# Input scaling of two layers moved to VectorE alone, norm vector loaded first, index heads paired with zero-padded keys

## The chip, the core and the metric

The kernel runs on one core of one Trainium2 chip. The metric is the device time of one execution in microseconds. The kernel before takes 2158.25 us (median of three executions, 2156.83 to 2161.36).

The engines of the core have these names in the profile: PE multiplies matrices (PEld are its weight loads), DVE is VectorE, ACT is ScalarE, POOL is GpSimd, SP issues most transfers.

## The reference

Input is one sequence of 256 tokens with 2048 features in fp32. Two layers follow each other. Each normalizes its input, makes one wide projection, runs two token mixers side by side, multiplies each by a gate, projects back and adds the result to the input.

```python
def layer_ab(x, ...):
    h = rms_norm(x, norm_g)                       # x * rsqrt(mean(x*x)) * gain
    proj = einsum('btd,de->bte', h, w_in)
    q, k, v, o_pre, z_a, i_pre, f_pre, z_b, xbc, dt_raw = split_cols(proj, SPLIT_AB)
    y = concatenate([mlstm_branch(...), mamba2_branch(...)])
    return x + einsum('bte,ed->btd', y, w_out)

def layer_cd(x, ...):
    h = rms_norm(x, norm_g)
    proj = einsum('btd,de->bte', h, w_in)
    q_c, ckv, z_c, iq, ik, iw, qkv, z_d, b_pre, a_pre = split_cols(proj, SPLIT_CD)
    y = concatenate([dsa_branch(...), gdn_branch(...)])
    return x + einsum('bte,ed->btd', y, w_out)
```

Inside `dsa_branch` every query scores all keys with 16 index heads of 64 features: `score = einsum('bqhd,bsd->bqhs', iq, ik)`, and `index = einsum('bqh,bqhs->bqs', iw, relu(score))` picks the keys that attention sees. `gdn_branch` is a gated delta rule over chunks of 64 tokens whose output is normalized head by head. A last rms_norm ends the program.

## The kernel before, in words

**Products in three parts.** Every projection keeps fp32 precision by splitting both operands into a high and a low part. A weight piece `wr` (four blocks of 128 rows by 512 columns, called a group here) arrives by DMA on SP's queue into one of three buffers. ACT casts it to `wh` (L191), DVE subtracts that from `wr` to get `wl` (L192); there are two buffers of each. The layer's input is held the same way in `hT`, transposed: 16 blocks k of 128 features, each with 256 high and 256 low columns. A product takes three matmuls for each pair of row block and column block: wh by high, wh by low, wl by high (`proj_feat`). A group is 48 such matmuls of 256 columns.

**What sets the order.** Small work is written as generators in the list `steps`. `tick()` advances the first of them by one `yield` and is called after each quarter of a group; `lag(n)` lets n ticks pass; `flush()` ticks until the list is empty. PE instructions issued inside a tick keep their place in program order, all others are placed by the tile scheduler by priority.

**The layer's input.** `normed()` turns the residual `xr` by PE (`xt`, L79), multiplies by the gain into `xg` (L306 on ACT, L308 on DVE), casts to the high half of `hT` (ACT, L295) and subtracts for the low half (L296: DVE for even pairs of blocks, POOL for odd). The squares are summed meanwhile (L323 on ACT, L325 on DVE), the inverse root is taken in 12 tiny DVE instructions (L141 to L147), spread over all partitions by `dg` (L333) and a product `rbp` with ones, and copied to `rb` (L335). The first product of a layer works on the unscaled `hT`, and its result is multiplied by `rb` when it leaves PSUM (L411 in layer 1, L747 in layer 2). After LR = 10 ticks the step `rescaled()` scales `hT` for all later products: eight times a DVE multiply of a pair of blocks (L315), an ACT cast (L295) and a POOL subtraction (L296). The first product of layer 1 is `bc_half(0)`, in groups of 1, 1, 2, 4, 4 and 4 blocks; after it come the gates' product, `bc_half(1)` and the other column blocks. In layer 2 the first is half of the index queries (CIQ, i = 0), then the other half.

**The other places.** `index()` computes the scores of one head a tick: two matmuls with the head's 64 features as contraction (128 and 256 columns). `delta()` ends with the normalization of the delta rule's output `og` on DVE (L1266), a lag of LT = 4 ticks and the turn of `og` by PE (L79). The turn of the normalized latent `cn` (L932) stands in the list without a lag. Matmuls `pw` have 64 columns of stationary operand.

## Time and profile before

| what | value |
|---|---|
| median of three executions | 2158.25 us (2156.83 to 2161.36) |
| profiled execution | 2157.74 us |
| its span, first to last instruction | 2156.0 us |
| PE busy | 2107.7 us, 98% |
| DVE, ACT, POOL busy | 1467.5, 993.7, 149.6 us |
| mean granted TensorE clock | 0.992 |

The page gives the busy time of each engine; the view of waits lists what the engine stood idle for; windows give the same busy times for chosen stretches with the granted clock (1.00 is the upper of the two levels, 0.50 the lower, values between are mixtures); the timeline lists runs of equal instructions with their start, and in brackets the idle time ahead of them and what ended it. Times count from the start of the span.

### The profile page before, as it was taken

How to read it: one execution, taken by the hardware profiler on the slowest of the kernel's cores; microseconds unless marked ns; L12 is line 12 of the kernel's file. 1: busy time of each engine (PE TensorE's matmuls, PEld its weight loads, DVE VectorE, ACT ScalarE, POOL GpSimd, SP SyncE). 2: the span in 40 equal slices, each digit the busy share in tenths (PEclk: the TensorE clock that was granted, in tenths of full speed). 3: DMA queues.
4: the chain of work that ended last, by engine and by line, in shares of the span. 5: the costliest groups of instructions: out<-in, count | busy, mean ns of one | idle time of the engine just before them, and what ended most of it. 6: DMA issues, size and time to landing. Idle time of an engine off the chain costs nothing.

```text
span 2156.0 us, 31526 instructions
## 1 busy us (share of the span) xinstructions
PE 2107.7 (98%) x12878; PEld 1861.2 (86%) x12878; DVE 1467.5 (68%) x2096; ACT 993.7 (46%) x1311; POOL 149.6 (7%) x168
## 2 busy tenths in 40 slices
PE   7999999999999999899999999999999999999997
PEld 6989997888889788898878888899898988989986
DVE  7888764555455456578979998555666666766765
ACT  5455443334433444355643333455444444444543
POOL 4000020000000000300100002000000000000001
PEclk9999999999999999999999999999999999999999
DMA  6565456555555555576886666755565555565543
GB/s 184 190 212 176 157 179 215 195 176 176 176 184 187 176 187 185 139 237 221 296 229 202 224 204 207 265 181 181 176 233 180 190 172 189 188 195 182 171 160 124
DMA packets 242342, 415.16 MB, mean 193 GB/s; under 512 B 45093, under 2 KB 69206, under 8 KB 240342
## 3 DMA queue, kind: packets, MB, share of 16 engines
q1 hardware_dynamic: 237254, 389.84, 55.4%
q0 software_dynamic: 4944, 23.31, 3.3%
q8 instruction: 101, 1.65, 0.3%
q14 instruction: 43, 0.35, 0.0%
HBM read 389.87 MB, written 26.38 MB: 193 GB/s over the span
## 4 chain that ended last, share of the span: by engine, by line
PE 85%; DVE 6%; ACT 3%; issue 1%; DMA 1%; ACTq 0%; SPq 0%
PE pt L75 49%; PE pf L75 27%; DVE wl L192 3%; ACT wh L191 2%; PE turn L79 1%; PE py L75 1%; PE pu L75 1%; PE si L75 1%; ACT Dt L862 1%; PE po L75 0%; PE lgt L75 0%; PE num L75 0%; PE pog L75 0%; DMA Dt<-gd 0%; PE vt L79 0%
## 5 line engine op out<-in xcount | busy, mean ns | idle before, releaser
L192 DVE TENSOR_TENSOR wl<-wr,wh 128x2048 fp32r<-128x2048 f32 (+1 forms) x337 | 777.1, 2306 | 482.6 <-ACT wh L191 479.1
L191 ACT CAST wh<-wr 128x2048 fp32r<-128x2048 f32 (+1 forms) x337 | 639.7, 1899 | 774.3 <-PE pt L75 455.4
L75 PE MATMUL pf<-hT,wh 128*128 128x256 f32 x4192 | 768.7, 285 | 0.3 <-POOL hT L296 0.2
L75 PEld LDWEIGHTS pf<-hT,wh 128*128 128x128 f32 x4192 | 650.2, 190 | 9.6 <-issue 5.7
L75 PE MATMUL pf<-hT,wl 128*128 128x256 f32 x2096 | 591.6, 283 | 14.6 <-DVE wl L192 14.6
L75 PE MATMUL pt<-wh,hT 128*128 128x512 f32 x1856 | 593.9, 398 | 0.0
L75 PEld LDWEIGHTS pt<-wh,hT 128*128 128x128 f32 x1856 | 349.2, 188 | 84.4 <-issue 1.9
L75 PEld LDWEIGHTS pf<-hT,wl 128*128 128x128 f32 x2096 | 398.2, 190 | 16.3 <-DVE wl L192 15.4
L75 PE MATMUL pt<-wl,hT 128*128 128x512 f32 x928 | 368.1, 397 | 1.3 <-DVE wl L192 1.3
L75 PE MATMUL pt<-wh,uc 128*128 128x512 f32 x768 | 250.4, 397 | 0.0
L75 PEld LDWEIGHTS pt<-wl,hT 128*128 128x128 f32 x928 | 174.7, 188 | 44.2 <-DVE wl L192 1.9
L75 PEld LDWEIGHTS pt<-wh,uc 128*128 128x128 f32 x768 | 143.9, 188 | 29.0 <-issue 0.5
L75 PE MATMUL pt<-wl,uc 128*128 128x512 f32 x384 | 151.2, 394 | 0.0
L381 DVE SCALAR_TENSOR_TENSOR cy<-pf,gconv,cy 128x255 f32<-128x255 f32 (+2 forms) x192 | 88.4, 477 | 5.3 <-ACT cy L377 3.1
L75 PEld LDWEIGHTS pt<-wl,uc 128*128 128x128 f32 x384 | 72.4, 188 | 13.6 <-DVE wl L192 0.4
L75 PE MATMUL pt<-wh,ua 128*128 128x512 f32 x256 | 80.0, 392 | 0.0
L75 PE MATMUL pt<-wh,ub 128*128 128x512 f32 x256 | 79.1, 389 | 0.0
L350 DVE TENSOR_TENSOR xr<-pt,xr 128x512 f32<-128x512 f32 x80 | 54.9, 686 | 25.5 <-PE pt L75 25.4
L75 PEld LDWEIGHTS pt<-wh,ub 128*128 128x128 f32 x256 | 48.1, 188 | 10.0
L1174 POOL TENSOR_TENSOR QD<-QD,qm 128x256 f32<-128x256 f32 x32 | 22.5, 739 | 491.7 <-DVE nrv L141 257.7
L75 PEld LDWEIGHTS pt<-wh,ua 128*128 128x128 f32 x256 | 47.9, 188 | 9.6
L296 POOL TENSOR_TENSOR hT<-xg,hT 128x512 fp32r<-128x512 f32 x24 | 40.8, 1711 | 201.7 <-issue 123.3
(457 smaller groups left out, 1868.8 us busy)
## 6 DMA issues: line engine op xcount, KB each, us to landing
wr<-in_cd_w_in_dram SPq DMA_DIRECT2D x140, 1024.0 KB, 5.1
wr<-in_ab_w_in_dram SPq DMA_DIRECT2D x87, 1024.0 KB, 5.2
wr<-in_cd_w_out_dram SPq DMA_DIRECT2D x48, 1024.0 KB, 5.1
wr<-in_ab_w_out_dram SPq DMA_DIRECT2D x32, 1024.0 KB, 5.1
wr<-in_ab_w_in_dram SPq DMA_DIRECT2D x33, 512.0 KB, 4.3
zd<-zk SPq DMA_DIRECT2D x12, 512.0 KB, 6.2
Dt<-gd SPq DMA_DIRECT2D x4, 1024.0 KB, 8.4
Dd<-Dt POOLq DMA_DIRECT2D x4, 1024.0 KB, 6.2
```

The source lines that it names most:

```text
L75: return held(nc.tensor.matmul(*args, **kw))
L79: return held(nc.tensor.transpose(*args, **kw))
L191: A.copy(wh[:, 0:nk, 0:n], wr[:, 0:nk, 0:n])
L192: V.tensor_tensor(wl[:, 0:nk, 0:n], wr[:, 0:nk, 0:n], wh[:, 0:nk, 0:n].bitcast(F32), op=OP.subtract)
L296: L.tensor_tensor(hT[:, both, 256:512], part, hT[:, both, 0:256].bitcast(F32), op=OP.subtract)
L350: V.tensor_tensor(xc, pts[t], xc, op=OP.add)
L381: V.scalar_tensor_tensor(yi[:, s:256], u[:, 0:256 - s], tap(3 - s), yi[:, s:256], op0=OP.mult, op1=OP.add)
L862: A.activation(dc, dc, AF.Abs, bias=ngc[:, c, i * 8 + h:i * 8 + h + 1])
L1174: G.tensor_tensor(QD[:, h], QD[:, h], qm[:, h // 2 * 256:h // 2 * 256 + 256], op=OP.mult)
```

## The change

**Start of layer 1.** The norm vector `gab_raw` and three of the four chunks of x are issued on ACT's queue, the first chunk on SP's. All eight pairs are turned first, squares and root follow at ordinary priority. **Scaling.** All splits are on DVE. The step `factor()` makes `rb` after 9 ticks (layer 1) or 6 (layer 2). A dictionary `scaling` lets one pair be scaled every second tick once its counter has run down, and `scaled_to()` forces a pair ahead of a product that needs it. In layer 1 `bc_half(0)`, the gates and `bc_half(1)` all work on unscaled `hT`; in layer 2 only the first product. **Index.** Keys are laid out with zeros so that one product serves two heads (256 and 512 columns). **Lags.** The turn of `og` waits 8 ticks instead of 4; that of `cn` 4 instead of none. **pw** gets 128 stationary columns, the last 64 of which are not used.

```diff
-LQ, LV, LS, LT = 5, 5, 2, 4
+LQ, LV, LS, LT, LO = 5, 5, 2, 4, 8
...
 LG, LG2, LK = 3, 6, 5
-LW, LR = 4, 10
+LW = 4
...
     xr = cp.tile([128, 2, D], F32, name="xr")
+    gab_raw = cp.tile([16, 128], F32, name="gab_raw")
+    nc.scalar.dma_start(gab_raw, ab_norm[0].rearrange("(b p) -> b p", p=128))
     for c in range(4):
-        nc.sync.dma_start(xr[:, :, c * 512:c * 512 + 512], x[:, c * 512:c * 512 + 512].rearrange("(t p) d -> p t d", p=128))
+        (nc.scalar if c else nc.sync).dma_start(xr[:, :, c * 512:c * 512 + 512], x[:, c * 512:c * 512 + 512].rearrange("(t p) d -> p t d", p=128))
...
     rows = lambda ap: ap.rearrange("(b p) -> b p", p=128)
-    gab = columns("gab", [(rows(ab_norm[0]), 16)], queue=G)
+    gab = cp.tile([128, 16], F32, name="gab")
+    gab_ps = mx("gab_ps")
+    transpose(gab_ps[:, 0:16], gab_raw)
+    V.tensor_copy(gab, gab_ps[:, 0:16])
...
     steps = []
+    scaling = {"gen": iter(()), "done": 8, "wait": None}
+    def scaled_to(n):
+        while scaling["done"] < n:
+            next(scaling["gen"], None)
+            scaling["done"] += 1
     def tick():
+        if scaling["wait"] is not None and scaling["done"] < 8:
+            scaling["wait"] -= 1
+            if scaling["wait"] <= 0:
+                scaled_to(scaling["done"] + 1)
+                scaling["wait"] = 2
...
         return pts
-    def proj_feat(src, r0, X, pieces, groups=None):
+    def proj_feat(src, r0, X, pieces, groups=None, raw=False):
...
                 xt, i = X[g + k]
+                if xt is hT and not raw:
+                    scaled_to(i // 2 + 1)
...
             pass
-    def normed(hT, gain, pool):
+    def normed(gain, pool, first, at):
...
         xg = [pool.tile([128, 8, 256], F32, name=f"xg{i}", tag=tag) for i, tag in enumerate(("Dt", "KD"))]
-        def split(i, L):
+        def split(i):
...
             A.copy(hT[:, both, 0:256], part)
-            L.tensor_tensor(hT[:, both, 256:512], part, hT[:, both, 0:256].bitcast(F32), op=OP.subtract)
+            V.tensor_tensor(hT[:, both, 256:512], part, hT[:, both, 0:256].bitcast(F32), op=OP.subtract)
...
                     V.tensor_scalar(dst, src, scalar1=g, scalar2=None, op0=OP.mult)
-            split(i, G if i % 2 else V)
+            split(i)
+        def squares(c):
+            xc = xr[:, :, c * 512:c * 512 + 512]
+            junk = wp.tile([128, 512], F32, name="junk", tag="cy", bufs=2)
+            A.activation(junk, xc[:, 0], AF.Square, accum_out=ss[:, 0, c:c + 1])
+            junk2 = wp.tile([128, 512], F32, name="junk2", tag="cy", bufs=2)
+            V.scalar_tensor_tensor(junk2, xc[:, 1], 1.0, xc[:, 1], op0=OP.mult, op1=OP.mult, accum_out=ss[:, 1, c:c + 1])
+        def root():
+            V.tensor_reduce(s1, ss, axis=mybir.AxisListType.X, op=OP.add)
+            rsqrt(rs, s1, 1.0 / D)
+            for t in range(2):
+                V.tensor_scalar(dg[:, t], ident, scalar1=rs[:, t:t + 1], scalar2=None, op0=OP.mult)
+        def factor():
+            yield from lag(at)
+            rbp = mx("rbp")
+            for t in range(2):
+                PE.matmul(rbp[:, t * 128:t * 128 + 128], ones, dg[:, t], start=True, stop=True)
+            A.copy(rb, rbp[:, 0:256])
         def rescaled():
-            yield from lag(LR)
...
                 V.tensor_tensor(both, both, rb.unsqueeze(1).to_broadcast([128, 2, 256]), op=OP.mult)
-                split(i, G)
+                split(i)
...
         with tc.high_priority():
+            if first:
+                for i in range(8):
+                    turned(i)
+            else:
+                for c in range(4):
+                    squares(c)
+                    if c:
+                        turned(c * 2 - 2)
+                        turned(c * 2 - 1)
+                root()
+                turned(6)
+                turned(7)
+        if first:
             for c in range(4):
...
+                squares(c)
+            root()
+        steps.append(factor())
+        scaling.update(gen=rescaled(), done=0, wait=None)
+        return [(hT, k) for k in range(16)], rb
...
         np1 = ExitStack()
-        X, rb = normed(hT, gab, np1.enter_context(tc.tile_pool(name="np1", bufs=1)))
+        X, rb = normed(gab, np1.enter_context(tc.tile_pool(name="np1", bufs=1)), True, 9)
+        rb2 = rb.unsqueeze(1).to_broadcast([128, 2, 256])
...
         def bc_half(i):
-            pts = proj_feat(ab_w_in, 0, X, [(AXBC + 2048 + i * 512, 512, 0)], None if i else [(0, 1), (1, 1), (2, 2), (4, 4), (8, 4), (12, 4)])
+            pts = proj_feat(ab_w_in, 0, X, [(AXBC + 2048 + i * 512, 512, 0)], None if i else [(0, 1), (1, 1), (2, 2), (4, 4), (8, 4), (12, 4)], raw=True)
...
             for b in range(2):
-                if i == 0:
-                    V.tensor_tensor(pair(pts[b]), pair(pts[b]), rb, op=OP.mult)
+                V.tensor_tensor(pair(pts[b]), pair(pts[b]), rb2, op=OP.mult)
...
         flush()
-        np1.close()
...
         gt = tmps.enter_context(tc.tile_pool(name="gt", bufs=1))
-        pts = proj_feat(ab_w_in, 0, X, [(AI, 4, 0), (AFG, 4, 28), (ADT, 32, 32)])
+        pts = proj_feat(ab_w_in, 0, X, [(AI, 4, 0), (AFG, 4, 28), (ADT, 32, 32)], raw=True)
         R = gt.tile([64, 256], F32, name="R")
-        A.copy(R, pts[0][0:64, 0:256])
+        V.tensor_tensor(R, pts[0][0:64, 0:256], rb[0:64], op=OP.mult)
...
         tmps.close()
+        scaling["wait"] = 4
         bc_half(1)
+        scaled_to(8)
+        np1.close()
...
         kq = kp.enter_context(tc.tile_pool(name="kq", bufs=1))
-        X, rb = normed(hT, gcol[:, G_CD:G_CD + 16], kq)
+        X, rb = normed(gcol[:, G_CD:G_CD + 16], kq, False, 6)
+        scaling["wait"] = 9
...
         for i in range(2):
-            pts = proj_feat(cd_w_in, 0, X, [(CIQ + i * 512, 512, 0)])
+            pts = proj_feat(cd_w_in, 0, X, [(CIQ + i * 512, 512, 0)], raw=i == 0)
...
                 if i == 0:
-                    V.tensor_tensor(dst, pair(pts[b]), rb, op=OP.mult)
+                    V.tensor_tensor(dst, pair(pts[b]), rb.unsqueeze(1).to_broadcast([128, 2, 256]), op=OP.mult)
...
         pts = proj_feat(cd_w_in, 0, X, [(CB, 64, 0), (CIW, 16, 64), (CIK, 64, 128), (CIK, 64, 192)])
-        ikT = qp.tile([128, 256], F32, name="ikT")
+        ikT = kq.tile([128, 2, 256], F32, name="ikT")
+        G.memset(ikT, 0.0)
...
         ssk = qp.tile([128, 2, 16], F32, name="ssk")
-        A.copy(ikT, pts[0][:, 256:512])
+        for b in range(2):
+            A.copy(ikT[b * 64:b * 64 + 64, b], pts[0][b * 64:b * 64 + 64, 256:512])
...
             iw = lambda t, h: RT[:, t, 64 + h:65 + h]
-            for h in range(h0, h0 + 8):
-                r = slice(h % 2 * 64, h % 2 * 64 + 64)
-                pt = mx("si")
-                PE.matmul(pt[:, 0:128], iqT[r, h // 2, 0:128], ikT[r, 0:128], start=True, stop=True)
-                PE.matmul(pt[:, 128:384], iqT[r, h // 2, 128:256], ikT[r], start=True, stop=True)
...
+            for h in range(h0, h0 + 8, 2):
+                p0, p1 = mx("si0"), mx("si1")
+                PE.matmul(p0[:, 0:256], iqT[:, h // 2, 0:128], ikT[:, :, 0:128], start=True, stop=True)
+                PE.matmul(p1, iqT[:, h // 2, 128:256], ikT, start=True, stop=True)
+                for r in range(2):
+                    tm = sc if h + r == 0 else kq.tile([128, 384], F32, name="tm", tag="tm", bufs=2)
+                    V.tensor_scalar(tm[:, 0:128], p0[:, r * 128:r * 128 + 128], scalar1=0.0, scalar2=iw(0, h + r), op0=OP.max, op1=OP.mult)
+                    V.tensor_scalar(tm[:, 128:384], p1[:, r * 256:r * 256 + 256], scalar1=0.0, scalar2=iw(1, h + r), op0=OP.max, op1=OP.mult)
+                    if h + r:
+                        V.tensor_tensor(sc, sc, tm, op=OP.add)
+                    yield
...
             A.activation(cn[:, t], pts[t], AF.Copy, scale=cr[:, t:t + 1])
-        steps.append(turning(cn, cT, 0, 4, [gcol[:, G_KV + i:G_KV + i + 1] for i in range(4)]))
+        def latent():
+            yield from lag(4)
+            yield from turning(cn, cT, 0, 4, [gcol[:, G_KV + i:G_KV + i + 1] for i in range(4)])
+        steps.append(latent())
...
             W1n = gp.tile([128, 4, 64], F32, name="W1n")
-            Bn = gp.tile([128, 4, 64], F32, name="Bn")
+            Bn = gp.tile([128, 5, 64], F32, name="Bn")
...
             nc.sync.dma_start(nr2, nrkd.rearrange("c p h -> (c p) h"))
+            G.memset(Bn[:, 4], 0.0)
...
                             PE.matmul(pb[:, m * 64:m * 64 + 64], KB[:, m], W1n[:, m], start=True, stop=True)
-                        V.tensor_tensor(Bn, pb[:, 0:256].rearrange("p (m j) -> p m j", m=4), nr2[:, h0:h0 + 4].unsqueeze(2).to_broadcast([128, 4, 64]), op=OP.mult)
+                        V.tensor_tensor(Bn[:, 0:4], pb[:, 0:256].rearrange("p (m j) -> p m j", m=4), nr2[:, h0:h0 + 4].unsqueeze(2).to_broadcast([128, 4, 64]), op=OP.mult)
...
                         for m in range(4):
-                            PE.matmul(pw[0:64, m * 128:m * 128 + 128], Bn[:, m], W2B[:, m], start=True, stop=True)
+                            PE.matmul(pw[:, m * 128:m * 128 + 128], Bn[:, m:m + 2], W2B[:, m], start=True, stop=True)
...
                             new_unit()
-                        yield from lag(LT)
+                        yield from lag(LO)
```

ACT at the program's start; `wh` is the first weight piece, `xg` the turned input, `junk` the squares, `neab` a vector of the Mamba branch. Before:

```order
L323 ACT_TABLE_LOAD
L323 ACTIVATE junk,ss<-xr 128x512 x4
L306 ACTIVATE xg_102<-xt,gab 128x256
L191 CAST wh<-wr 128x512 x2
L306 ACTIVATE xg_102<-xt,gab 128x256 x3
L295 CAST hT<-xg_102 128x2x256 x3
```

and of the changed kernel:

```order
L97 DMA gab_raw<-in_ab_norm_dram 16x128
L99 DMA xr<-in_x_dram 128x2x512 x3
L210 ACT_TABLE_LOAD
L210 CAST wh<-wr 128x512 x2
L336 ACTIVATE junk,ss<-xr 128x512
L471 ACTIVATE neab<-neab 128x32
L336 ACTIVATE junk,ss<-xr 128x512
L328 ACTIVATE xg_102<-xt,gab 128x256 x3
L336 ACTIVATE junk,ss<-xr 128x512
L317 CAST hT<-xg_102 128x2x256 x3
```

The two weight casts and `neab` now stand ahead of the first `xg` and the first cast of `hT`.

DVE at the start of layer 2, from the spreading of the root to the eviction of the first product (`iqT`). Before:

```order
L333 TENSOR_SCALAR dg<-ident,rs 128x128 x2
L192 TENSOR_TENSOR wl<-wr,wh 128x2048
L308 TENSOR_SCALAR xg_6709<-xt,gcol 128x256 x2
L315 TENSOR_TENSOR xg_6708<-xg_6708,rb 128x512
L296 TENSOR_TENSOR hT<-xg_6709,hT 128x2x256
L315 TENSOR_TENSOR xg_6708<-xg_6708,rb 128x512 x3
L315 TENSOR_TENSOR xg_6709<-xg_6709,rb 128x512 x3
L192 TENSOR_TENSOR wl<-wr,wh 128x2048
L315 TENSOR_TENSOR xg_6709<-xg_6709,rb 128x512
L192 TENSOR_TENSOR wl<-wr,wh 128x2048
```

and of the changed kernel:

```order
L344 TENSOR_SCALAR dg<-ident,rs 128x128 x2
L211 TENSOR_TENSOR wl<-wr,wh 128x2048
L356 TENSOR_TENSOR xg_6710<-xg_6710,rb 128x512 x3
L318 TENSOR_TENSOR hT<-xg_6710,hT 128x2x256
L356 TENSOR_TENSOR xg_6710<-xg_6710,rb 128x512
L356 TENSOR_TENSOR xg_6711<-xg_6711,rb 128x512
L211 TENSOR_TENSOR wl<-wr,wh 128x2048
L318 TENSOR_TENSOR hT<-xg_6710,hT 128x2x256 x3
L318 TENSOR_TENSOR hT<-xg_6711,hT 128x2x256
L356 TENSOR_TENSOR xg_6711<-xg_6711,rb 128x512
L211 TENSOR_TENSOR wl<-wr,wh 128x2048
```

Between the first and the second `wl` stood seven multiplies and one split; now five multiplies and one split, and the splits that POOL did follow among the next pieces.

PE at the first turn of a delta output `og`. Before:

```order
L75 MATMUL pf_13649<-hT,wh 128x256 x2
L79 MATMUL turn<-ident,og__13474 128x128
L75 MATMUL pf_13649<-hT,wl 128x256
L75 MATMUL pf_13649<-hT,wh 128x256 x2
L75 MATMUL pf_13649<-hT,wl 128x256
```

and of the changed kernel:

```order
L75 MATMUL pf_13639<-hT,wh 128x256 x2
L75 MATMUL pf_13639<-hT,wl 128x256
L79 MATMUL turn<-ident,og__13463 128x128 x8
L75 MATMUL pq<-qc,kT 128x128 x4
L75 MATMUL pb<-W1n,KB 128x64 x4
L75 MATMUL pt_13986<-wh,uc_12503 128x512
```

The turn stood within the last quarter groups of a product; now its eight matmuls stand together behind that product, four ticks later.

## Rows read from the trace of the kernel before

**Rows 1.** The page: span; busy time, share and instructions of PE.

```profile
span 2156.0 us, 31526 instructions
...
PE 2107.7 (98%) x12878; PEld 1861.2 (86%) x12878; DVE 1467.5 (68%) x2096; ACT 993.7 (46%) x1311; POOL 149.6 (7%) x168
```

**Rows 2.** Waits of PE: us in total, times, longest.

```profile
PE pf L75 <- DVE wl L192: 14.6, 4, 6.0
PE gab_ps L79 <- DMA gab_raw<-in_ab_norm_dram: 7.1, 1, 7.1
PE xt L79 <- ACT xg L306: 2.3, 2, 2.0
PE turn L79 <- ACT cn L932: 2.0, 1, 2.0
PE rbp L75 <- DVE dg L333: 1.9, 1, 1.9
...
PE turn L79 <- DVE og__13474 L1266: 0.6, 1, 0.6
```

**Rows 3.** Timeline of PE, layer 1's first product: start, us, instructions, [idle before].

```profile
14.23 0.99 PE L75 MATMUL pf<-hT,wh 128*128 128x256 f32 x3
...
43.13 0.38 PE L75 MATMUL pf<-hT,wl 128*128 128x256 f32 x1 [3.70 <-DVE wl L192]
```

**Rows 4.** Groups of DVE, 0 to 51 us: busy us, mean ns.

```profile
L315 DVE TENSOR_TENSOR xg<-xg,rb 128x512 f32<-128x512 f32 x8 | 11.6, 1504 | 0.0
L192 DVE TENSOR_TENSOR wl<-wr,wh 128x2048 fp32r<-128x2048 f32 x4 | 10.2, 2547 | 0.0
```

**Rows 5.** Timeline of DVE, last eviction of layer 1's first product.

```profile
50.36 0.70 DVE L411 TENSOR_TENSOR pf<-pf,rb 128x512 f32<-128x512 f32 x1 [2.15 <-PE pf L75]
```

**Rows 6.** Timeline of ACT, first casts of the input.

```profile
13.06 1.66 ACT L295 CAST hT<-xg 128x512 fp32r<-128x512 f32 x3 [0.20 <-DVE xg L308]
```

**Rows 7.** Windows: PE, PEld, DVE, ACT, POOL busy (instructions), granted clock, DMA share, GB/s.

```profile
45.00:50.00 5.00, 5.00 (x35) 5.00 (x35) 2.76 (x2) 0.30 (x1) 0.00 (x0) 0.76 0.84 286
...
880.00:885.00 5.00, 5.00 (x30) 5.00 (x30) 2.32 (x2) 0.00 (x0) 0.00 (x0) 0.63 0.99 339
...
86.00:92.00 6.00, 6.00 (x53) 5.53 (x52) 5.81 (x12) 2.30 (x3) 0.54 (x1) 1.00 0.58 193
```

**Rows 8.** Timeline of DVE, start of layer 2.

```profile
864.08 0.68 DVE L315 TENSOR_TENSOR xg<-xg,rb 128x512 f32<-128x512 f32 x1
864.68 0.68 DVE L296 TENSOR_TENSOR hT<-xg,hT 128x512 fp32r<-128x512 f32 x1
865.28 10.28 DVE L315 TENSOR_TENSOR xg<-xg,rb 128x512 f32<-128x512 f32 x6
...
879.35 2.28 DVE L192 TENSOR_TENSOR wl<-wr,wh 128x2048 fp32r<-128x2048 f32 x1
```

**Rows 9.** Timeline of POOL, same stretch.

```profile
865.02 4.91 POOL L296 TENSOR_TENSOR hT<-xg,hT 128x512 fp32r<-128x512 f32 x3 [16.05 <-ACT hT L295]
```

**Rows 10.** Timeline of PE, same stretch.

```profile
878.88 0.58 PE L75 MATMUL pf<-hT,wl 128*128 128x256 f32 x1 [6.03 <-DVE wl L192]
```

**Rows 11.** Timeline of PE, last product of one delta output.

```profile
1641.76 1.06 PE L75 MATMUL pog<-u,QD 128*128 128x128 f32 x8
```

**Rows 12.** Timeline of DVE, normalization of that output.

```profile
1648.80 2.19 DVE L1266 SCALAR_TENSOR_TENSOR og__13474<-og__13474,ysc,zg 128x128 f32<-128x128 f32 x8
```

**Rows 13.** Windows from 940 to 1100 us, index scores alone: sums, then means.

```profile
sum 160.00, PE 14.71 PEld 8.28 DVE 12.26; mean PE 1.84 PEld 1.03 DVE 1.53
```

**Rows 14.** Groups of PE by form: busy us, mean ns of one.

```profile
L75 PE MATMUL num<-v,P 128*128 128x512 f32 x24 | 11.6, 592 | 0.0
L75 PE MATMUL pw<-W2B,Bn 128*64 128x128 f32 x64 | 8.7, 279 | 0.0
L75 PE MATMUL pq<-qc,kT 128*128 128x128 f32 x64 | 8.4, 275 | 0.0
L75 PE MATMUL pqs<-S,qc 128*128 128x256 f32 x32 | 8.2, 379 | 0.0
```

More of the change, by code (lines that the diff above doesn't have):

```diff
@@ L315, in rescaled @@
                 V.tensor_tensor(both, both, rb.unsqueeze(1).to_broadcast([128, 2, 256]), op=OP.mult)
-                split(i, G)
+                split(i)
                 yield
         with tc.high_priority():
-            for c in range(4):
-                xc = xr[:, :, c * 512:c * 512 + 512]
-                junk = wp.tile([128, 512], F32, name="junk", tag="cy", bufs=2)
-                A.activation(junk, xc[:, 0], AF.Square, accum_out=ss[:, 0, c:c + 1])
-                junk2 = wp.tile([128, 512], F32, name="junk2", tag="cy", bufs=2)
-                V.scalar_tensor_tensor(junk2, xc[:, 1], 1.0, xc[:, 1], op0=OP.mult, op1=OP.mult, accum_out=ss[:, 1, c:c + 1])
-                if c:
-                    turned(c * 2 - 2)
-                    turned(c * 2 - 1)
-            V.tensor_reduce(s1, ss, axis=mybir.AxisListType.X, op=OP.add)
-            rsqrt(rs, s1, 1.0 / D)
-            rbp = mx("rbp")
-            for t in range(2):
-                V.tensor_scalar(dg[:, t], ident, scalar1=rs[:, t:t + 1], scalar2=None, op0=OP.mult)
-                PE.matmul(rbp[:, t * 128:t * 128 + 128], ones, dg[:, t], start=True, stop=True)
-            A.copy(rb, rbp[:, 0:256])
-            turned(6)
-            turned(7)
-        steps.append(rescaled())
-        return [(hT, k) for k in range(16)], rb.unsqueeze(1).to_broadcast([128, 2, 256])
+            if first:
[11 more added lines that the diff above has]
+        if first:
+            for c in range(4):
+                squares(c)
[3 more added lines that the diff above has]
+        return [(hT, k) for k in range(16)], rb
     pair = lambda pt: pt.rearrange("p (k t) -> p k t", k=2)
@@ L816, in index @@
             iw = lambda t, h: RT[:, t, 64 + h:65 + h]
-            for h in range(h0, h0 + 8):
-                r = slice(h % 2 * 64, h % 2 * 64 + 64)
-                pt = mx("si")
-                PE.matmul(pt[:, 0:128], iqT[r, h // 2, 0:128], ikT[r, 0:128], start=True, stop=True)
-                PE.matmul(pt[:, 128:384], iqT[r, h // 2, 128:256], ikT[r], start=True, stop=True)
-                tm = sc if h == 0 else kq.tile([128, 384], F32, name="tm", tag="tm", bufs=2)
-                V.tensor_scalar(tm[:, 0:128], pt[:, 0:128], scalar1=0.0, scalar2=iw(0, h), op0=OP.max, op1=OP.mult)
-                V.tensor_scalar(tm[:, 128:384], pt[:, 128:384], scalar1=0.0, scalar2=iw(1, h), op0=OP.max, op1=OP.mult)
-                if h:
-                    V.tensor_tensor(sc, sc, tm, op=OP.add)
-                yield
+            for h in range(h0, h0 + 8, 2):
[9 more added lines that the diff above has]
+                    yield
         def top():
```

## The prediction

> **What bounds the kernel now.** I read the page first. PE is busy 2107.7 of 2156.0 us [rows 1], so time can come from two places only: the 48.3 us in which PE stands idle, and PE's own busy time, where it does needless work or runs at the lower clock. The waits of PE show the first. The largest are four waits of a product for its low weight part `wl`, 14.6 us together, the longest 6.0; then 7.1 for the norm vector at the start, and small ones: 2.3 for the first turned inputs, 2.0 for the latent `cn`, 1.9 for `dg`, and 0.6 for a delta output, a row that stands for six equal ones [rows 2]. Timeline and windows then say where these lie. The 3.70 us wait is the end of layer 1's first product [rows 3], the 6.03 us wait the first product of layer 2 [rows 10]. The other two lie elsewhere (0.8 us early in the first product, some 4 us near 1345 us, which the change does not touch).
>
> Both long waits have one cause. In layer 2 one multiply alone takes 0.60 us from start to start, and so does a subtraction; while POOL does the splits of the same pairs, six multiplies take 10.28 us, 1.7 each [rows 8, 9]. `wl` stands behind them. In layer 1 the eight multiplies cost 11.6 us [rows 4] against 8 x 0.60 = 4.8 alone. A wait also leaves the clock low: 0.63 after the wait in layer 2, 0.76 after the one in layer 1 [rows 7], a mixture of 1.2 and 2.4 GHz.
>
> **The change part by part.** Sums are made against the profiled execution, 2157.74 us, of which 2156.0 are span; it lies 0.5 us below the median of the runs.
>
> *Start of layer 2.* DVE no longer shares the stretch with POOL. It now does eight splits more, 4.8 us at 0.60. The order shows five multiplies and one split between the two pieces that were 6.03 us apart from PE's need: 6 x 0.60 = 3.6 instead of 10.28 + 0.60. At the pace of one pair every second tick, two pairs fall on a group: 4 x 0.60 + 2.28 for `wl` = 4.7 us of DVE, against 5.4 us of PE at least (48 matmuls; 53 are recorded in 6 us at the upper clock [rows 7], a few may be missing). So the wait should go, with about 0.7 us to spare. The clock loss goes with it: 0.37 of the 5 us from 880, and some 0.3 of the last microsecond before: 2.2 us. Together -8.2. Bounds: -8.2, as nothing more is lost there, and +3 if DVE is late at the first of the pieces and again at the next.
>
> *Start of layer 1.* The same multiplies go through DVE without POOL, and the last wait of 3.70 and the clock loss after it (0.24 x 5 = 1.2) should go. Four earlier splits and a `dg` were stretched as well, which a split's 0.60 and the plain instructions of the root put at about 2.6 together. Against this the product starts later. ACT's first rows are now the casts of the two first weight pieces, squares and `neab`, which waits for a vector that is transferred behind the weights; the first cast of the input, at 13.06 before [rows 6], comes behind two squares of 0.7, and `neab`, some 1.5 us later. The wait of 7.1 us for the norm vector [rows 2] was hidden: the product also wants weights and x, and began only at 14.23 [rows 3]. `dg` is still waited for, in the order its matmul stands behind nine ticks while the root's tiny instructions are spread among the splits, so its 1.9 us is left as it is. Net -3.7 - 1.2 - 2.6 + 1.5 = -6.0. Layer 1's first product should then leave PSUM near 44 instead of 50.4 [rows 5]. Bounds: -11.7 (3.7 + 1.2 + the whole 6.8 by which the multiplies were stretched) and +1 (all of the gains, and the product 8.5 us late).
>
> The Trainium skill's page "DMA: Bandwidth & Descriptors" (Issuing engines are not separate DMA queues) says that transfers issued by different engines run on the same 16 DMA engines and interleave, so a second issuing engine saves issue time alone. By that rule x, which had the queue to itself ahead of the weights, now shares with them, which speaks against the change; it would make the first product later, not earlier, and is the mechanism of the first rival below.
>
> *Later in layer 1.* The splits of pairs now fall into `bc_half(1)` and what follows. New DVE work there: 8 x 0.60 for the splits, two evictions of 0.70 [rows 5], and 0.4 for the gates: 6.6 us. DVE is already busy 5.81 of 6 us from 86 to 92, while PE is at 6.00 and the clock at 1.00 [rows 7], so cover is thin. I take +1.5, a quarter of it, since the splits begin earlier, in groups where DVE has room; bounds 0 and +6.6, all of it on the path.
>
> *Delta output.* Six turns wait 0.6 us each [rows 2]. The normalization runs from 1648.80, 2.19 us [rows 12], 7 us after the last product of the output at 1641.76 [rows 11]; by the matmuls counted in the order, at 0.113 each, the turn came some 6 us after it and now comes some 11 us after it. -3.5; bounds -3.5 and 0 (the wait is short, no clock loss stands beside it). Its results are wanted later than that by the output projection, whose matmuls in between are other units'.
>
> *Index.* The 16 heads cost PE 14.71 us [rows 13], 1.84 for two. Now 256 and 512 columns at full contraction: `pqs`, 8.2 us for 16 products of 256 columns (each is two records), is 0.51; `num`, 11.6 for 12 of 512, is 0.97 [rows 14]. 8 x 1.48 = 11.8, so -2.9; bounds -3.2 and 0 (the same 768 columns at the price of before). DVE does the same work per head. The zero fill on POOL has a whole product before anyone wants it.
>
> The Trainium skill, "TensorE: Matmul & The Clock Gate", Why this matters for your kernels, says that a small-contraction matmul takes as long as a full one, and that the gain of small ones is to run side by side in distinct row groups. By that rule the padding gains nothing (768 columns either way), and the sum would be 2.9 us higher. The rows disagree so far: 1.84 against 1.48 for equal columns; and the heads here stand in different ticks, so no two ever ran side by side.
>
> *No effect.* `pw` gets 128 stationary columns: `pq` has them and costs 275 ns a record against 279 [rows 14], so nothing, within 0.3. The lag on `cn` leaves its turn at the same place in PE's order, behind the first products of the last group, so its 2.0 us wait [rows 2] stays.
>
> **The sum:** -8.2 - 6.0 + 1.5 - 3.5 - 2.9 = -19.1; 2157.7 - 19.1 = 2138.6, and against the median 2139.
>
> **The rivals.**
> 1. *The start gives nothing.* ACT holds the first casts for weights and for `neab`, x arrives among weights, and the product starts 6 us later than I reckon. For it: ACT is in order, and 3.70 us of wait were the whole visible loss there. Against: the multiplies' 11.6 us really shrink. 2139 + 6 = 2145.
> 2. *`wl` stays late in layer 2.* A split follows an ACT cast that must itself wait until PE has read the unscaled block; DVE is in order, so `wl` behind it is held. Spare is only 0.7 us a group. A wait of 3 and the 2.2 of clock stay: 2139 + 5 = 2144.
> 3. *More than I booked.* The start gives 11 instead of 6 and the crowding costs nothing: 2139 - 5 - 1.5 = 2132.5.
> 4. *Slower: DVE becomes the bound.* Place: `bc_half(1)` and the blocks after it, and the second product of layer 2. It decides if DVE needs over 5.4 us a group: 4.7 in layer 2, near 5.8 of 6 in layer 1. Then 6.6 + 4.8 = 11.4 us of moved work land on PE's path, in some five gaps, each with 2.2 us of low clock, 11; layer 2's 8.2 are not won: 2158.2 - 6.0 - 3.5 - 2.9 + 11.4 + 11 = 2168. Against: POOL's sharing, the dearest part of DVE's time here, is gone.
> 5. *It doesn't do what it says.* The `cn` lag is such a case already. If `scaled_to` rather than the counter sets the pace, the pairs come in a burst at the second product: about 4 us of DVE work at once, 2143.
>
> **How the numbers follow.** Forecast 0.57 (2133 to 2145), start without gain 0.14, `wl` late 0.08, burst 0.04, more than booked 0.12, slower 0.05. The range that leaves out no more than 2 in 10 is 2129 to 2148; it takes in the first three rivals and, of the bounds, all but the two extremes. A measurement tells 0.2%, 4.3 us, from no change. Only rival 4 is slower; a mixture of rivals 1, 2 and crowding can end within 4.3 us. Faster 0.92, same 0.04, slower 0.04.
>
> **What would show it.** In the waits of PE the 6.03 and 3.70 rows are gone and the clock is 1.00 from 875 us on (shifted); L356 takes 0.60 from start to start; no POOL L318. The eviction of the first product stands near 44. The six delta waits are gone, the `cn` wait of 2.0 stays. The index scores sum to about 11.8 us. DVE over 5.9 of 6 us with new waits for `wl` between 50 and 100 us, or after the first product of layer 2, would make the forecast wrong; so would a first product after 18 us.

## The result, and the profile after

The changed kernel takes 2130.59 us (median of four, 2127.67 to 2131.46) against 2157.54 (four, 2155.99 to 2161.36) of the kernel before: ratio 0.987, 95% interval 0.9853 to 0.9887, 27 us faster. The forecast was 2139, in a range of 2129 to 2148: right in sign and inside the range, and 8 us too cautious. The profiled execution of the changed kernel took 2131.35 us.

The page, span and busy times (before: [rows 1]):

```profile
span 2129.6 us, 31469 instructions
...
PE 2091.1 (98%) x12846; PEld 1851.9 (87%) x12846; DVE 1456.8 (68%) x2123; ACT 992.4 (47%) x1311; POOL 115.6 (5%) x145
```

PE's idle time fell from 48.3 to 38.5 us, 9.8 of the 26.4 us of span. The other 16.6 us are busy time; where they lie is shown below. The waits of PE in the changed kernel (before: [rows 2]); columns are us in total, times, longest:

```profile
PE pf L75 <- DVE wl L211: 5.0, 3, 4.1
PE pt L75 <- DVE wl L211: 4.7, 4, 1.8
PE gab_ps L79 <- DMA gab_raw<-in_ab_norm_dram: 3.6, 1, 3.6
PE xt L79 <- ACT xg L328: 3.4, 1, 3.4
PE xt L79 <- DMA xr<-in_x_dram: 2.9, 2, 1.5
PE si L75 <- DVE tm L869: 1.7, 1, 1.7
PE turn L79 <- ACT cn L978: 1.4, 1, 1.4
```

The waits of 6.03 and 3.70 us are gone, and so are the 1.9 for `dg` and the six for `og`; the 4.1 us one is the old one (ended at 1352 us before, at 1336 now), outside the change. The rows of `gab_ps` and `xt` lie ahead of the first product. New are the 1.7 for the index sums (`si`) and, in the second row, 1.8 for a `wl` near 1032 us. A list of waits can't show busy time, so the two traces were laid beside each other at ACT's 337 weight casts, which come in the same order in both. The time between equal casts:

| from the start, up to cast | what it is | before | after | difference | forecast |
|---|---|---|---|---|---|
| 8 | layer 1's first product | 50.2 | 43.4 | -6.8 | -6.0 |
| 25 | rest of layer 1's front | 108.4 | 109.7 | +1.4 | +1.5 |
| 141 | layer 1 | 695.1 | 695.5 | +0.5 | 0 |
| 145 | start of layer 2 | 32.9 | 23.7 | -9.2 | -8.2 |
| 173 | index scores and keys | 188.0 | 187.6 | -0.4 | -2.9 |
| 222 | latent and attention | 285.9 | 283.6 | -2.3 | 0 |
| 337 | delta rule | 773.1 | 763.7 | -9.4 | -3.5 |

Each column is one profile, and the profiles of the experiments show how far the same code differs. The start of layer 2 takes 23.7 and the delta rule 763.5 to 763.7 in all that leave them as they are. The first row is 42.1 to 43.4 in eight profiles of the changed start, the second 108.5 to 111.7, the third 694.0 to 696.4, the index row 184.9 to 187.9. Differences of a us or two in these rows are not clear of that spread.

At the start of layer 2, DVE's timeline (start, us, instructions, idle before; before: [rows 8]):

```profile
860.29 1.90 DVE L356 TENSOR_TENSOR xg<-xg,rb 128x512 f32<-128x512 f32 x3 [0.93 <-ACT rb L351]
862.11 0.68 DVE L318 TENSOR_TENSOR hT<-xg,hT 128x512 fp32r<-128x512 f32 x1
862.71 1.29 DVE L356 TENSOR_TENSOR xg<-xg,rb 128x512 f32<-128x512 f32 x2
863.91 2.28 DVE L211 TENSOR_TENSOR wl<-wr,wh 128x2048 fp32r<-128x2048 f32 x1
866.11 2.49 DVE L318 TENSOR_TENSOR hT<-xg,hT 128x512 fp32r<-128x512 f32 x4
```

and the windows of the same stretch (PE, PEld, DVE, ACT, POOL busy, clock, DMA share, GB/s; before: [rows 7]):

```profile
865.00:870.00 5.00, 5.00 (x45) 5.00 (x45) 5.00 (x7) 3.08 (x4) 0.00 (x0) 1.00 0.50 159
870.00:875.00 5.00, 5.00 (x46) 5.00 (x45) 5.00 (x7) 2.58 (x3) 0.00 (x0) 1.00 0.63 207
```

A multiply takes 0.60 again instead of 1.7, PE doesn't stop, and the clock stays at its upper level. DVE is full there, and fast enough that no wait appears. The start was held where the forecast put it: ACT waits for the transfer of `neab` ahead of the first `xg` (timeline of ACT; before: [rows 6]).

```profile
12.67 0.23 ACT L471 ACTIVATE neab<-neab 128x32 f32<-128x32 f32 x1 [3.05 <-DMA neab<-in_ab_ssm_a_log_dram]
12.80 0.61 ACT L336 ACTIVATE junk<-xr 128x512 f32<-128x512 f32 x1
13.32 0.19 ACT L336 ACTIVATION_READ_ACCUMULATOR junk<-xr 128x1 f32 x1
13.42 1.18 ACT L328 ACTIVATE xg<-xt,gab 128x256 f32<-128x256 f32 x3
```

The first product begins at 16.03 us, 1.8 later than at 14.23 [rows 3], and its last eviction still begins at 43.53 instead of 50.36 [rows 5].

### The profile page after: what moved, and what is told of

Its sections match the earlier page's. It is cut to its first block, busy times and chain, and to the rows that moved or that the text cites. A ratio compares the mean times of both kernels' runs of the same rounds, so it can differ in the third digit from the quotient of the medians.

```text
span 2129.6 us, 31469 instructions
## 1 busy us (share of the span) xinstructions
PE 2091.1 (98%) x12846; PEld 1851.9 (87%) x12846; DVE 1456.8 (68%) x2123; ACT 992.4 (47%) x1311; POOL 115.6 (5%) x145
## 4 chain that ended last, share of the span: by engine, by line
PE 90%; DMA 4%; DVE 4%; ACT 2%; issue 1%; ACTq 0%; SPq 0%
PE pt L75 48%; PE pf L75 32%; DVE wl L211 2%; ACT wh L210 1%; PE py L75 1%; DMA Dt<-gd 1%; PE turn L79 1%; DMA wr<-in_ab_w_in_dram 1%; DMA wr<-in_cd_w_in_dram 1%; PE pog L75 1%; PE pu L75 1%; PE po L75 1%; PE lgt L75 0%; PE num L75 0%; ACT Dt L908 0%
## 5 line engine op out<-in xcount | busy, mean ns | idle before, releaser
L1226 POOL TENSOR_TENSOR QD<-QD,qm 128x256 f32<-128x256 f32 x32 | 30.5, 986 | 474.6 <-DVE qm L1223 241.0
L1019 DVE TENSOR_TENSOR U<-U,tmp 128x62 f32<-128x62 f32 (+30 forms) x62 | 53.1, 857 | 1.2
```

The lines of the kernel that those rows point to most:

```text
L1019: V.tensor_tensor(U[:, 0:s, s + 1:64], U[:, 0:s, s + 1:64], tv, op=OP.subtract)
L1226: G.tensor_tensor(QD[:, h], QD[:, h], qm[:, h // 2 * 256:h // 2 * 256 + 256], op=OP.mult)
```

## The experiments

Every kernel but one (it says so) is the changed one with the edit shown, without lines that only follow from it ("..." marks a cut). Stretches are given between casts as above.

**The lag of the delta output.**

```diff
-LQ, LV, LS, LT, LO = 5, 5, 2, 4, 8
+LQ, LV, LS, LT, LO = 5, 5, 2, 4, 4
```

> The changed kernel with the turn of the delta output og after 4 ticks again instead of 8; nothing else differs. In PE's order the turn's eight matmuls are scattered again among the last products, one, two, one and four at a time. Theory A (the stretch of the delta rule gained about 9 us because the lag removed six waits of 0.6 us and the scattering as well, and pw's padding about 2): the six waits of 0.6 come back and PE pays about 2.5 us more for the scattered turns, so about +6 us, some 2137. Rival B (the lag is worth the listed waits alone): +3.5 us, some 2134. Rival C (the stretch gained for another reason, the turn's place does not matter): 2131.

2137.53 us (four, 2135.82 to 2141.47). The delta stretch takes 770.4 instead of 763.7, +6.7: theory A. PE's timeline at the first turn, with four ticks again:

```profile
1629.50 0.30 PE L79 MATMUL turn<-ident,og__13463 128*128 128x128 f32 x1 [0.60 <-DVE og__13463 L1318]
1629.56 0.36 PE L75 MATMUL pf<-hT,wl 128*128 128x256 f32 x1
...
1630.46 0.43 PE L79 MATMUL turn<-ident,og__13463 128*128 128x128 f32 x2
1630.65 0.37 PE L75 MATMUL pf<-hT,wh 128*128 128x256 f32 x1
1630.86 0.27 PE L79 MATMUL turn<-ident,og__13463 128*128 128x128 f32 x1
```

and in the changed kernel:

```profile
1636.60 1.03 PE L79 MATMUL turn<-ident,og__13463 128*128 128x128 f32 x8
1637.47 1.06 PE L75 MATMUL pq<-qc,kT 128*128 128x128 f32 x8
```

Of the 6.7, the six waits are 3.6, and waits of the next unit's first turn (`qt`, 1.4 us with four ticks, 0.2 with eight) are 1.2. Some 2 us are left that no wait in the list shows. The scattering came back with them, but whether it costs them was not tested apart from the lag.

**The columns of pw.**

```diff
-PE.matmul(pw[:, m * 128:m * 128 + 128], Bn[:, m:m + 2], W2B[:, m], start=True, stop=True)
+PE.matmul(pw[0:64, m * 128:m * 128 + 128], Bn[:, m], W2B[:, m], start=True, stop=True)
...
```

> The changed kernel with the product pw on 64 stationary columns again. Theory A (PE loses about 0.1 us on going from a product of 128 stationary columns to one of 64 and about 0.17 us on the way back, eight times): +2.2 us, some 2133, and the steps from pw to the next product read 0.20 us again instead of 0.03. Rival B (the prediction: the padding is worth nothing): within 0.3 us of the changed kernel on the stretch of the delta rule.

2131.96 us (2131.64 to 2133.61); the delta stretch is 765.8, +2.1, as theory A says. The means per record are what the forecast read, 279 against 274 ns (groups of PE, with 64 columns and then, changed, with 128):

```profile
L75 PE MATMUL pw<-W2B,Bn 128*64 128x128 f32 x64 | 8.7, 279 | 0.0
```

```profile
L75 PE MATMUL pw<-W2B,Bn 128*128 128x128 f32 x64 | 8.4, 274 | 0.0
```

The cost stands between the records. PE's timeline at the first place, with 64 columns and then with 128:

```profile
1579.19 0.28 PE L75 MATMUL pf<-hT,wl 128*128 128x256 f32 x1
1579.40 1.09 PE L75 MATMUL pw<-W2B,Bn 128*64 128x128 f32 x8
1580.42 0.51 PE L75 MATMUL pf<-hT,wh 128*128 128x256 f32 x2
```

```profile
1580.93 0.28 PE L75 MATMUL pf<-hT,wl 128*128 128x256 f32 x1
1581.05 1.05 PE L75 MATMUL pw<-W2B,Bn 128*128 128x128 f32 x8
1581.86 0.48 PE L75 MATMUL pf<-hT,wh 128*128 128x256 f32 x2
```

From the start of the product before to the start of the one behind it is 1.23 us against 0.93. From the last `pw` to the next product it is 0.20 us at all eight places with 64 columns, with 128 it is 0.03 at four and 0.11 at the other four (`vt` follows there); from a product into `pw` 0.21 or 0.32 against 0.12 or 0.23.

**One index head per product.** The loop over heads, the key layout and its copies are those of the kernel before.

```diff
...
-PE.matmul(p0[:, 0:256], iqT[:, h // 2, 0:128], ikT[:, :, 0:128], start=True, stop=True)
-PE.matmul(p1, iqT[:, h // 2, 128:256], ikT, start=True, stop=True)
+PE.matmul(pt[:, 0:128], iqT[r, h // 2, 0:128], ikT[r, 0:128], start=True, stop=True)
+PE.matmul(pt[:, 128:384], iqT[r, h // 2, 128:256], ikT[r], start=True, stop=True)
...
```

> The changed kernel with the index scores one head per product again (64 rows of contraction, 128 and 256 columns). Theory A: the scores cost PE 2.1 us for two heads instead of 1.3 (+6.4), but the new wait of 1.74 us for the first sums goes, and so may the wait of 1.83 us for wl near 1032 us with the low clock behind it (1.7): +1 to +5 us. Rival B (the prediction's price, 1.84 against 1.48 for two heads): +2.9 us less 1.7, +1.2. Rival C (the wait at 1032 us comes from the transfer of Dt and not from the scores): it stays, and the kernel is +4.7 us.

2133.29 us (2129.53 to 2133.76). From cast 145 to 165, where the scores are, it takes 136.6 us against 132.5: pairing saves 4.1 net of the 1.74 wait, so about 5.8 on PE, twice the forecast: theory A's price and not rival B's. From 165 to 168 it takes 19.7 against 23.3: the changed kernel gives 3.6 back there (2.8 in its second profile), so that the whole index row is 188.6 against 187.6, and the ratios' intervals overlap. Rival C is out, since the wait at 1032 us goes with the pairing. The scores' records in the changed kernel (before: [rows 13]):

```profile
sum 160.00, PE 12.48 PEld 5.11 DVE 11.93; mean PE 1.56 PEld 0.64 DVE 1.49
```

They sum to 2.2 us less than before; the forecast named a sum of 11.8 as a sign. The rest of the saving stands between records. From start to start PE takes, with one head, 0.21 us into its first record, 0.21 and 0.11 for the two records of 128 columns, 0.22 and 0.31 for those of 256, and 0.22 for the first record of the product behind. Less the 0.12 that the product's own records take elsewhere, that is 2.1 us for two heads, against 1.3 for a pair in one product. That it is the 64 rows and not the number of products is seen from `pw` with 128 columns above: eight short records of full height in 0.81 us, with no long step ahead of them. ACT's timeline, changed kernel:

```profile
1027.88 0.40 ACT L908 ACTIVATE Dt<-Dt,ngc 128x128 f32<-128x128 f32 x1 [6.21 <-DMA Dt<-gd]
1028.18 1.89 ACT L210 CAST wh<-wr 128x2048 fp32r<-128x2048 f32 x1
```

and with one head per product:

```profile
1025.73 1.91 ACT L210 CAST wh<-wr 128x2048 fp32r<-128x2048 f32 x1 [3.07 <-PE pt L75]
1029.07 3.62 ACT L906 ACTIVATE Dt<-Dt,ngc 128x128 f32<-128x128 f32 x12 [0.90 <-DMA Dt<-gd]
```

The pairing moved one `Dt` activation ahead of a weight cast on ACT. It waits 6.2 us for its transfer, the cast with it, `wl` is 1.83 us late, and the clock is at 0.66 from 1033 to 1038 us.

**neab out of the way,** then the same again beside the changed kernel.

```diff
+late = mp.tile([128, 1], F32, name="late")
+V.tensor_scalar(late, rb[:, 0:1], scalar1=0.0, scalar2=None, op0=OP.mult)
-A.activation(nea[:, 4:36], nea[:, 4:36], AF.Exp)
+A.activation(nea[:, 4:36], nea[:, 4:36], AF.Exp, bias=late)
```

> The changed kernel with the exponential of neab made to wait for rb (one tiny VectorE instruction more), so that it no longer stands on ScalarE ahead of the first turned input. Theory A (ScalarE's 3.05 us wait for that vector's transfer holds the first xg and with it the first product): the first product starts about 3 us earlier, near 13 instead of 16.03, and the first product's last eviction is about 3 us earlier than 43.5; some 2128. Rival B (x and weights, or VectorE's casts and differences, set the start): the first product starts earlier but the eviction stays near 43; 2131.

> The changed kernel itself, beside the other runs of this call: 2131 within 2 us, by both theories. It says how far one profile of the same kernel differs from another, above all up to the first product's last eviction (43.4 us in the first profile, 42.1 to 42.8 in the runs that left the start as it is).

> The kernel with neab late once more, five rounds, to settle whether it beats the changed kernel. Theory A (ScalarE's wait for the neab transfer costs the start about 3 us): 2126 within 1.5, the interval of its ratio below the changed kernel's middle. Rival B (the earlier difference was the spread of runs): 2130 or more.

2125.74 us (2123.80 to 2128.59), ratio 0.9856 (0.9841 to 0.9871); again 2126.86 (2126.11 to 2127.85), ratio 0.9855 (0.9834 to 0.9876), beside 2130.23 (2128.76 to 2131.17), ratio 0.9869 (0.9848 to 0.9891), for the changed kernel. The intervals of the ratios overlap, and the second one reaches above the changed kernel's middle, so that run alone does not settle it. Taken together, the eight executions with `neab` late average 2126.4 us (2123.80 to 2128.59), the nine of the changed kernel 2130.1 (2127.67 to 2131.46), 3.6 us apart. The first product begins 3.0 us earlier (PE):

```profile
13.06 0.78 PE L75 MATMUL pf<-hT,wh 128*128 128x256 f32 x2
```

and cast 8 comes at 39.6 and 40.1 instead of 43.4 and 42.8 (42.1 at the earliest in any profile of the changed start). Theory A. The second profile of the changed kernel also shows the spread: near 1032 us it waits 1.1 us for `wl` instead of 1.8, and no low clock follows.

**All of x on SP's queue.**

```diff
-(nc.scalar if c else nc.sync).dma_start(xr[:, :, c * 512:c * 512 + 512], ...)
+nc.sync.dma_start(xr[:, :, c * 512:c * 512 + 512], ...)
```

> The changed kernel with all four chunks of x on SP's queue ahead of the weights as before; the norm vector stays on ScalarE's queue, issued first. ScalarE's order then also has neab behind the first casts. Theory A (queues do not matter, all transfers share the same engines; what held the start of the changed kernel is ScalarE's wait for neab): the first product starts near 13 to 14 us and its last eviction near 40, as in the run with neab late. Rival B (the second queue brings x and weights together and is worth something): the first weight piece lands near 10.6 as before instead of 6, the first product starts at 14.2, and the eviction is at 41 or later. Rival C (the start gained by the early norm vector alone): as A.

2127.10 us (2126.18 to 2132.16); first product at 13.71, cast 8 at 39.7, as with `neab` late on two queues. The edit also takes `neab` from ahead of the first `xg` in ACT's order, so the comparison is with that run and not with the changed kernel. Theory A: the second queue is worth nothing that can be seen here.

**The splits back on POOL, then the pace.**

```diff
-def split(i):
+def split(i, L=V):
...
-    V.tensor_tensor(hT[:, both, 256:512], part, hT[:, both, 0:256].bitcast(F32), op=OP.subtract)
+    L.tensor_tensor(hT[:, both, 256:512], part, hT[:, both, 0:256].bitcast(F32), op=OP.subtract)
...
-split(i)
+split(i, G)
```

> The changed kernel with the subtractions of the rescaled pairs (not of the raw ones) on POOL again, in both layers, at the new pace and places. Theory A (at the start of layer 2 the long wait came from DVE and POOL working at the same time, multiplies of 1.7 us instead of 0.60): POOL's splits now overlap DVE's, the instructions beside them stretch, and a wait for wl with low clock behind it comes back in layer 2's first product: +5 to +9 us there. Rival B (it came from the burst, eight pairs at once ahead of wl, and the new pace alone cures it): the stretch stays at 23.7 us, within 0.5. In layer 1 (90 to 153 us) the theory of the crowded VectorE says that 4.8 us less of its work give back most of the 2.2 us lost there; if sharing costs more than the moved work, it gets worse.

2136.68 us (2135.31 to 2138.02), +6.1. The start of layer 2 takes 26.5 instead of 23.7, less than theory A asked, more than rival B; PE waits 2.5 us for `wl` there (and 0.8 just behind), and its clock stays at 1.00. From cast 8 to 16, where layer 1's splits are (55.7 to 84.6 us), it takes 50.4 instead of 46.5. The crowded VectorE gets worse, not better, when 4.8 us of its work move away. DVE beside POOL:

```profile
863.14 5.91 DVE L356 TENSOR_TENSOR xg<-xg,rb 128x512 f32<-128x512 f32 x6 [0.93 <-ACT rb L351]
868.97 3.37 DVE L211 TENSOR_TENSOR wl<-wr,wh 128x2048 fp32r<-128x2048 f32 x1
872.27 3.46 DVE L356 TENSOR_TENSOR xg<-xg,rb 128x512 f32<-128x512 f32 x2
```

```diff
-scaling["wait"] = 2
+scaling["wait"] = scaling.get("step", 2)
...
-scaling["wait"] = 9
+scaling["wait"] = 11
+scaling["step"] = 1
```

> The changed kernel with layer 2's pairs scaled one a tick from the eleventh tick on, as the kernel before counted, instead of one every second tick from the ninth; all on VectorE. VectorE's order is the same row by row up to the third wl of the stretch and differs by one place behind it. Theory A (POOL's splits and what they do to the order and to the instructions beside them are the cause, the pace matters little since the scheduler draws the multiplies forward anyway): the boundary takes 23.7 us within 0.3, and the kernel 2131 within 2. Rival B (the pace of one pair every second tick is what keeps wl in time): 25 us or more, with a wait for wl.

2130.64 us (2128.54 to 2132.38), boundary 23.74 us: no difference. Between these two paces the pace is not the cause. An earlier try at the same question told nothing:

```diff
-scaled_to(scaling["done"] + 1)
+scaled_to(8 if scaling.get("burst") else scaling["done"] + 1)
...
+scaling["burst"] = True
```

> The changed kernel with layer 2's eight pairs scaled all at once when the counter has run down (tick 9), all on VectorE, instead of one pair every second tick. VectorE's order then has ten multiplies and splits between the second and the third wl there, where the changed kernel has five. Theory A (the pace is what keeps wl in time): ten times 0.60 and a wl of 2.28 are 8.3 us against 5.4 to 5.6 for the group, so wl is late by up to 2.8 us, less what it was ahead, and low clock follows: +1 to +5 us on the stretch of the boundary, 23.7 before. Rival B (POOL's sharing was the whole cause, and eight pairs on VectorE alone are cheap enough): 23.7 within 0.3.

2136.78 us, boundary 32.0. In this kernel the first product of layer 2 takes its last blocks already scaled, which changes what it computes, and PE waits for them (2.9 for ACT's cast, 2.6 for the split), not for `wl`. It tests neither theory.

**One word in the kernel before.** Here the base is the kernel before.

```diff
-                split(i, G)
+                split(i, V)
                 yield
```

> The kernel before, with one word changed: the eight splits of the rescaled pairs are on VectorE instead of POOL, at the old places and the old pace (in the list of steps, one a tick after ten ticks). Everything else is as before. Theory A (two VectorE-heavy stretches were lost to VectorE and POOL working at the same time, so the choice of engine alone brings most of it): the boundary takes 23.7 to 25 us instead of 32.9 and layer 1's first product ends 4 to 7 us earlier than at 50.2: some 2142 to 2146. Rival B (the choice of engine is worth the 2.7 us that the run with POOL's splits showed, and the new place and pace of the pairs the rest): the boundary takes about 30 us.

2146.30 us (2145.36 to 2147.33), ratio to the kernel before 0.9952 (0.9936 to 0.9969). Cast 8 comes at 43.2 instead of 50.2, as in the changed kernel, and the boundary takes 24.5 instead of 32.9: theory A. These two stretches win 15.5 us in the profiles and the whole span 12.1; 1.1 are lost between casts 8 and 25, and 2.7 between 25 and 141, where a wait for `wl` near 338 us is longer (1.8 for 1.3) and the clock behind it lower (0.66 from 338 to 343 us). DVE at the boundary:

```profile
864.29 0.68 DVE L315 TENSOR_TENSOR xg<-xg,rb 128x512 f32<-128x512 f32 x1
864.89 0.68 DVE L296 TENSOR_TENSOR hT<-xg,hT 128x512 fp32r<-128x512 f32 x1
865.50 1.28 DVE L315 TENSOR_TENSOR xg<-xg,rb 128x512 f32<-128x512 f32 x2
866.70 2.28 DVE L192 TENSOR_TENSOR wl<-wr,wh 128x2048 fp32r<-128x2048 f32 x1
```

**A step beyond.** `neab` late, and room for the index sums:

```diff
                         V.tensor_tensor(sc, sc, tm, op=OP.add)
                     yield
+                if h0 == 0:
+                    yield
```

> The run with neab late, and in addition one empty tick after each of the first four pairs of index heads. In ScalarE's order the lone first activation of Dt then no longer stands ahead of a weight cast. Theory A (the index pairs gained 4 us on PE and gave most of it back: 1.74 us in a wait of the fourth pair for the sums of the second, which still hold its buffers, and about 3.5 in the wait for wl near 1032 us behind ScalarE's 6.2 us wait for the transfer of Dt): both waits go, and the stretch from the second to the end of the keys' products is 3.5 to 5 us shorter than in the changed kernel. With neab late: some 2122. Rival B (the waits only move, since the transfer of Dt takes its 9 us anyway and VectorE is as busy): 2126, as with neab late alone.

2125.10 us (2124.84 to 2126.24), ratio 0.9854 (0.9840 to 0.9869). Both waits go: casts 165 to 168 take 19.5 instead of 23.3. A wait of 1.1 for another `wl` comes at 960 us. But the wait for `cn` (1.7) is now followed by the lower clock, as in the kernel before (0.66 from 1063 to 1068 us), `kt` waits 1.3, and the total equals that of `neab` late alone. Rival B. These two are the fastest versions found, 3 to 5 us below the changed kernel.

## Why the prediction was right, and where it was off

- **Start of layer 2 (-8.2, measured -9.2).** The mechanism was right: POOL beside DVE stretched the multiplies, and one word in the kernel before brings 8.5 of the 9.2. No wait came, as the spare of 0.7 us a group said; DVE is busy in all of 865 to 875 us, so how much of the spare was left isn't shown. The forecast took its two pairs a group from the pace; twice that pace changes nothing. In the new order POOL's splits cost 2.7 (a wait of 2.5, no low clock), where they cost 8.5 in the old one (a wait of 6.0 and low clock behind it). What in the order makes that difference wasn't separated. The Trainium skill's page "SBUF — State Buffer" (two separate sides) says that VectorE with two SBUF inputs and GpSimd take turns for a whole instruction at a shared port. The trace agrees: from 866 to 875 us (records of [rows 8, 9]) the ends of the two engines' instructions alternate, a multiply ends 0.55 us after a split and the next split 1.15 us after the multiply, 1.7 together.
- **Start of layer 1 (-6.0, measured -6.8).** The wait of `neab` stood where the forecast put it; the product began 1.8 us later where 1.5 was booked, and without `neab` it begins 3.0 earlier. Two terms were off on the side of the gains. "`dg` is still waited for ... so its 1.9 us is left as it is" failed: the product with `dg` now stands at 34.4 us instead of 26.8, PE doesn't wait for it, and the clock of 0.70 from 25 to 30 us is 1.00. And of the "four earlier splits" booked as stretched, two were (1.38 and 1.78 us against 0.68). The sum came near with these errors in it. With splits on VectorE alone and no other change the product ends as early as in the changed kernel (cast 8 at 43.2), so the early norm vector, the second queue and the new order of squares bring nothing net as they stand. Rival 1 is out.
- **Later in layer 1 (+1.5, measured +1.4, with the row of layer 1 +1.9).** The size came near by luck; the step failed: "New DVE work there: ... cover is thin". The splits lie at 55.7 to 84.6 us, and the stretch that holds them, casts 8 to 16, became 0.9 shorter (46.5 for 47.4). The loss is behind it: casts 16 to 25 take 63.2 for 61.0. PE has three waits there that the kernel before has not, 0.75 and 0.63 for `wl` (at 114 and 125 us) and 1.0 ahead of `xst` (123 us). Ahead of them DVE stands idle 2.15 us for the transfer of `Ab`, and the instructions that follow it sit in front of `wl`. That this wait is the cause was not tested, and the same code took 62.0 to 65.2 in other profiles. With the splits on POOL it took 62.5, within that spread.
- **Delta output (-3.5, measured -6.7)** and **pw (0, measured -2.1)**, together the largest miss. "-3.5; bounds -3.5 and 0" counted listed waits alone. They are six of 0.6, 3.6 us; the lag also cleared 1.2 us of `qt` waits and about 2 us that no listed wait shows. And "`pq` has them and costs 275 ns a record against 279 ..., so nothing" compared durations of records, where the cost lay between them.
- **Index (-2.9, measured -0.4 in its stretch, -2.2 in the second profile).** The term was too small on PE (5.8 instead of 2.9, since records leave out what 64 rows cost between them) and blind to what follows: a wait of 1.7 for buffers and the displaced `Dt`, 3.6. The Trainium skill's rule that the prediction set against this term ("TensorE: Matmul & The Clock Gate", Why this matters for your kernels), no gain from padding, isn't borne out: the same 768 columns cost about 0.7 us less a pair. The Trainium skill's rule on queues, set against the start of layer 1 ("DMA: Bandwidth & Descriptors", Issuing engines are not separate DMA queues), is: x on one queue or two, cast 8 comes at 39.7 or 39.6.
- **cn (0).** The wait stayed, 1.4 for 2.0. The lower clock behind it (0.66 from 1085 to 1090 us before) is gone in all profiles of the changed order but the last run's; it is part of the 2.3 us of the latent row, which nothing booked. The lag of `cn` isn't shown to be the reason: in the kernel before with splits on VectorE, which has no such lag, `cn` waits 1.7 and the clock stays at 1.00, too.
- **Slower (rival 4).** It needed DVE over 5.4 us a group; PE shows no wait for `wl` from 850 to 890 us, and none between casts 8 and 16.
- **More than booked (rival 3, 2132.5).** Its time is nearer to the measured one than the forecast's, but not its path: the start gave 7 us and not 11. What came on top of the forecast are the delta rule with `pw` (5.9), the latent row (2.3) and 1.8 at the two starts, less 2.5 of the index. The long wait of rival 2 didn't come, and of rival 5 only the `cn` lag.

## What to carry to other kernels

Two engines that slow each other can be worth less than one of them alone, as DVE and POOL were here: look for an instruction whose duration varies between places before splitting work by engine. Read what a kind of matmul costs from the start of the product before it to the start of the product after it, not from its records. A piece that gets faster moves its neighbours in the order: ask which in-order engine will now wait first, as ACT did for `neab` and for `Dt`.

## What the runs showed that was not expected

- Going from products with 128 stationary columns to 64 and back costs PE 0.30 us where a product of 256 or 512 columns follows (1.23 against 0.93 at the place shown) and some 0.22 where one of 128 follows. Four of each make the 2.1 us measured.
- The lower clock doesn't follow every wait of one length. After a `cn` wait of 1.7 us it fell to 0.66 in the last run above, and not at all after one of 1.7 in the run with one head per product (windows as above, in this order):

```profile
1063.00:1068.00 5.00, 5.00 (x19) 4.12 (x19) 3.15 (x6) 2.34 (x5) 0.40 (x1) 0.66 1.03 147
1069.00:1074.00 5.00, 5.00 (x26) 4.14 (x25) 2.77 (x6) 3.67 (x6) 0.11 (x1) 1.00 1.03 153
```
